# First attention: the scores of two heads in one step, with two half-height matmuls

## The chip, the cores and the metric

The kernel runs on one core of a Trainium2 chip. The time is the device time of one execution in microseconds, and lower is better. The core has a matrix engine (PE, TensorE), with its weight loads shown apart as PEld, two engines for elementwise work (DVE, ACT), a third, slower one (POOL), and queues that start DMA transfers (SP's and ACT's here). Each engine works through its own list of instructions in order and waits for the others through semaphores. Matmuls write to PSUM banks of 128 partitions by 512 floats; DVE and ACT read them from there.

## What is computed

One encoder layer for 1024 tokens of width 1024. A normed input goes through one projection whose columns feed two attentions, their outputs go through one output projection, and a gated MLP with a convolution of width 3 follows. The change touches only the scores of the first attention: windows of 128 tokens to either side, eight query heads of 64 dimensions, two key heads, and a learned sink per head:

```python
qa = partial_rope(qa.reshape(B, S, A_HEADS, HEAD_DIM), cos, sin)
ka = partial_rope(ka.reshape(B, S, A_KV_HEADS, HEAD_DIM), cos, sin)
...
s = jnp.einsum('bqgrd,bkgd->bgrqk', q_i, k_i).astype(jnp.float32) * scale
s = jnp.where(valid[None, None, None], s, -1e30)
m = jnp.maximum(jnp.max(s, axis=-1), sink_gr)
p = jnp.exp(s - m[..., None])
denom = jnp.sum(p, axis=-1) + jnp.exp(sink_gr - m)
o = jnp.einsum('bgrqk,bkgd->bgrqd', p.astype(v_i.dtype), v_i)
o = o / denom[..., None].astype(o.dtype)
```

## The kernel before

**Numbers in two parts.** Each operand of a matmul is split into a high part (a copy rounded to the matmul's type) and a low part (what the copy lost). A projection step is three matmuls, high weights by high input, high weights by low input, low weights by high input (`block`, L189 to L192).

**Scores.** A head has 64 dimensions, half of the array's 128 rows, so the high and the low part of a query are stacked in one tile of 128 partitions. A key is kept as two such tiles, one with high above low and one with low above high (`split_first_k` and `split_k`). `scores` (L398) multiplies the query's tile by both: the first matmul gives high by high plus low by low, the second the two mixed products, both into one bank `s`. Two heads come out of one projection tile; `split_first` (group 0) and `split_pair` (group 1) make their query tiles. In group 0 the second head has low above high already; in group 1 both have high above low, the halves being put in place by three copies on SP's queue.

**Tiling.** A unit is one key head (group `g` of four query heads) and one block `b` of 128 queries; there are 16 (`unit_window`, L461). Its scores are 128 by 384 for each head, or 128 by 256 in the first and last block of a group. A unit has four `q_step`s, one for a head, and two or three `t_step`s, one for a block of keys.

- A `q_step` takes a bank `s` (there are two), issues the two matmuls and calls `softmax`: DVE adds the mask and takes the minimum of the negated scores (L435), and the exponential on ACT (L443) is put off until the next call of `exponentials`, that is until the next `softmax` or the next `t_step`. After the second head of a pair, DVE inverts both sums (L445) and POOL scales both tiles (L447).
- A `t_step` transposes the four heads' blocks on TensorE (L483), splits the result into a high part on ACT (L457) and a low part on DVE (L458), and leaves a `v_step` of two matmuls (L489, L490), which is run one `t_step` later.

**Order.** TensorE's list is written out by hand: its instructions run in the order of the program. The loop over units takes the steps of the unit's transposes and, between them, the `q_step`s of the unit two further on (positions `EVA`). After each step it adds a share of other work (`fill`): projection products for later stages, in the number given by `RATES`. The order on DVE and ACT is left to a scheduler, with the softmax and the split of the transposes at raised priority.

Of the kernel before, what the change touches and what calls it, by code (L numbers as in the profile page):

```python
# [58 lines left out]
def hybrid_layer(tc, xT, w_first, w_in, w_out, w_gate, w_up, w_down, small, sink, rpb, consts, rope, out):  # L59
    nc = tc.nc  # L60
    with ExitStack() as ctx:
# [23 lines left out]
        def big(name, tag, dt=F32):  # L85
            return lpool.tile([128, S], dt, name=name, tag=tag, bufs=slots[tag])
# [4 lines left out]
        def bank(name, tag):  # L91
            return psum.tile([128, HALF], F32, name=name, tag=tag)

        f32 = lambda ap: ap.bitcast(F32)
# [21 lines left out]
        for name, dst, n in (("h", his, 2), ("h", his, 2), ("l", los, 2), ("l", los, 2), ("w", None, 2)):  # L116
            t = flat(big(name, "mix", F32R)[:, :], n)
# [47 lines left out]
        def behind(*names):  # L165

            stack = ExitStack()
            for n in names:
                stack.enter_context(tc.issue_after(mark[n].ins))
            return stack  # L170
# [108 lines left out]
        def split_pair(t):  # L279

            a, b = big("q", "op", F32R), big("q", "op", F32R)
            lo = t[:, :].bitcast(F32R)
            for h in range(2):
                nc.scalar.activation(a[:, tsl(h)], t[:, tsl(h)], AF.Copy, scale=-HD ** -0.5)
                nc.vector.scalar_tensor_tensor(lo[:, tsl(h)], t[:, tsl(h)], -HD ** -0.5, f32(a[:, tsl(h)]), op0=ALU.mult, op1=ALU.subtract)
            nc.sync.dma_start(f32(b[0:64, :]), f32(a[64:128, :]))
            nc.sync.dma_start(f32(b[64:128, :]), t[64:128])
            nc.sync.dma_start(f32(a[64:128, :]), t[0:64])
            return [a, b]

# [31 lines left out]
        def split_k(t, e):  # L322

            a, b = big("ka", "op", F32R), big("kb", "op", F32R)
            o = 64 - e
            nc.scalar.activation(a[e:e + 64], t[e:e + 64], AF.Copy)
            nc.sync.dma_start(f32(b[o:o + 64, :]), f32(a[e:e + 64, :]))
            nc.vector.tensor_tensor(b[e:e + 64], t[e:e + 64], f32(a[e:e + 64, :]), op=ALU.subtract)
            nc.sync.dma_start(f32(a[o:o + 64, :]), f32(b[e:e + 64, :]))
            return a, b  # L330

        later = []

# [28 lines left out]
        qa, ka, va, qb, kb, vb = {}, {}, {}, {}, {}, {}  # L362
# [32 lines left out]
        def near(b):  # L395
            return [c for c in (b - 1, b, b + 1) if 0 <= c < NB]

        def scores(q, k, b):  # L398
            cs = near(b)
            n = 128 * len(cs)  # L400
            ps = bank("s", "s")
            qs = q[:, b * 128:(b + 1) * 128]
            for i in range(2):
                nc.tensor.matmul(ps[:, 0:n], qs, k[i][:, cs[0] * 128:cs[0] * 128 + n].rearrange("p (s w) -> p w s", s=2), start=i == 0, stop=i == 1)  # L404
            return ps, n
# [4 lines left out]
        def pair_tile(spare=False):  # L410
            pairs[0] += 1
            if spare and pairs[0] % 7 in SPARE:
                return lpool.tile([128, 2, 386], F32, name="p", tag="mix", bufs=slots["mix"], padded_shape=[128, 2, 512])
            return apool.tile([128, 2, 386], F32, name="p", tag="p", bufs=5, padded_shape=[128, 2, 392])
# [3 lines left out]
        def exponentials(*order):  # L418
            while deferred:
                with tc.high_priority(offset=50):  # L420
                    deferred.pop(0)(*order)

        def softmax(st, j, ps, n, bias, nsink=None):

            exponentials()
            w = lambda ap: ap.rearrange("p (s w) -> p s w", s=2)
            p = st["p"]
            with tc.high_priority(offset=50):
                nm = spool.tile([128, 1], F32, name="nm")
                if j == 0:  # L430
                    st["sm"], st["n"] = spool.tile([128, 2], F32, name="sm"), [n, n]
                sm, st["n"][j] = st["sm"], n
                if nsink is not None and j == 0:
                    nc.gpsimd.tensor_copy(p[:, 0:2, n:n + 1], nsink.rearrange("p (j o) -> p j o", o=1))
                nc.vector.tensor_tensor_reduce(  # L435
                    out=w(p[:, j, 0:n]), in0=ps[:, 0:n].rearrange("p (w s) -> p s w", s=2), in1=bias, scale=1.0, scalar=3e38 if nsink is None else nsink[:, j:j + 1],
                    op0=ALU.add, op1=ALU.min, accum_out=nm)
                e = n if nsink is None else n + 1
                widths = list(st["n"])

                def finish(*order):
                    with behind(*order):
                        nc.scalar.activation(p[:, j, 0:e], p[:, j, 0:e], AF.Exp, bias=nm, scale=-1.0, accum_out=sm[:, j:j + 1])  # L443
                    if j == 1:
                        nc.vector.reciprocal(sm, sm)  # L445
                        for i, m in enumerate(widths):
                            mark["scaled"] = nc.gpsimd.tensor_scalar(p[:, i, 0:m], p[:, i, 0:m], sm[:, i:i + 1], 1.0, op0=ALU.mult, op1=ALU.mult)  # L447

                deferred.append(finish)
                if nsink is None:  # L450
                    exponentials()
# [9 lines left out]
        def unit_window(g, b):  # L461

            cs, n = near(b), 128 * len(near(b))
            ps4 = [None] * 4
            mask = w2(cst[:, K_MA + 128 * (cs[0] - b + 1):K_MA + 128 * (cs[-1] - b + 2)])
            st = {}

            def q_step(j):
                def go():
                    if j % 2 == 0:  # L470
                        st["p"] = pair_tile(True)
                    ps, _ = scores(qa[g, j // 2][j % 2], ka[g], b)
                    softmax(st, j % 2, ps, n, mask, nsink[:, 4 * g + j - j % 2:4 * g + j - j % 2 + 2])
                    ps4[j] = st["p"][:, j % 2, :]
                return go

            def t_step(i):
                def go():
                    if i == 0:
                        st["o"] = bank("o", "o")  # L480
                    pt = bank("pt", "pt")
                    for j in range(4):
                        nc.tensor.transpose(pt[:, j * 128:(j + 1) * 128], ps4[j][:, i * 128:(i + 1) * 128], ident)  # L483
                    ph, pl = split_pt(pt, HALF)
                    exponentials("high")

                    def v_step():
                        o, v = st["o"], va[g]
                        nc.tensor.matmul(o, v[:, cs[i], :], mv(ph[:, :]), start=i == 0, stop=False)  # L489
                        nc.tensor.matmul(o, v[:, cs[i], :], mv(pl[:, :]), start=False, stop=i == len(cs) - 1)  # L490
                        if i == len(cs) - 1:
                            leave()
                    return v_step
                return go

            def leave():
                ot = apool.tile([128, 2, 128], F32, name="ot", tag="ot", bufs=1, padded_shape=[128, 4, 128])
                o4 = pv(st["o"][:, :])
                halved = lambda ap: ap.rearrange("p (s w) -> p s w", s=2)
                for e in range(2):  # L500
                    me, other = slice(64 * e, 64 * e + 64), slice(64 - 64 * e, 128 - 64 * e)
                    nc.scalar.activation(ot[me].rearrange("p j (s w) -> p j s w", s=2), o4[other, e::2], AF.Copy)
                    for i in range(2):
                        if mix[2 * g + i] is None:
                            mix[2 * g + i] = big("mixa", "mix")
                        nc.vector.tensor_tensor(halved(mix[2 * g + i][me, b * 128:(b + 1) * 128]), o4[me, e + 2 * i], halved(ot[me, i, :]), op=ALU.add)

            return [q_step(j) for j in range(4)], [t_step(i) for i in range(len(cs))]
# [220 lines left out]
        nsink = cpool.tile([128, 8], F32, name="nsink")  # L729
# [5 lines left out]
        t = quarters(big("f", "mix"))  # L735
# [15 lines left out]
        for part in range(3):  # L751
            for p, ps in zip(first, banks):
                w, x = p.w[0], xg[0]
# [55 lines left out]
        def second_k():  # L809
            ka[1] = split_k(first[0].t, 64)  # L810
# [74 lines left out]
        for g in range(2):  # L885
            for b in range(NB):
                q, t = unit_window(g, b)
# [59 lines left out]
        for u in range(len(flat)):  # L947
            q, t, need, kind = flat[u]
# [123 lines left out]
        at = lambda k, h: h1[k][:, tsl(h)]  # L1072
# [48 lines left out]
        for h in range(2):  # L1121
            for d in range(KT):
                if h == 0 and d + 2 < KT:
                    wo.append(load_wo(d + 2, False))
                ps = bank("pj", ("o", "s", "pj")[(h * KT + d) % 3])
# [438 lines left out]
        for i, (p, j, c) in enumerate(order):  # L1564
# [4 lines left out]
            f, n = PARTS[c]  # L1569
# [5 lines left out]
            ps = banks[p, j]  # L1575
# [8 lines left out]
            q = i % 12  # L1584
# [18 lines left out]
        for k, cols in enumerate(quarters):  # L1603
            for j in (2, 3):
                ps = banks[6, j]
# [116 lines left out]
```

## Time and profile before

| | before |
|---|---|
| median of 3 runs | 1014.34 us (1014.22 to 1014.41) |
| span of the profiled execution | 1012.1 us |
| matmuls, weight loads | 5080, 5080 |
| HBM read, written | 104.11 MB, 28.58 MB |
| score matmuls of both attentions (L404) | 128 with each key tile |

The profiled execution's own time is not shown apart; its span, from the first to the last instruction, is 2.24 us under the median of the runs.

How to read a row: a group's row has line, engine, operation, output and inputs, shapes and count, then busy time in us, the mean of one in ns, and the idle time ahead with what ended it. A row of the timeline has start, duration, engine, line, operation and count. Matmuls are pipelined: a row's duration overlaps with the next one's, so the distance between two starts tells what a matmul takes of the stream.

### The profile page before, as it was taken

The numbers are of one execution on the slowest core, as the hardware profiler recorded it, in microseconds if no ns is written. First come the engines' busy times: TensorE is split into PE (matmuls) and PEld (weight loads), VectorE is DVE, ScalarE is ACT, GpSimd is POOL, SyncE is SP. The second block draws the span as 40 slices with busy tenths as digits, with TensorE's granted clock in tenths as the row PEclk, the third lists the DMA queues.
The fourth block names the chain that finished last, engine by engine and source line by source line (L and its number), as shares of the span: only waits on it lengthen the run. The fifth ranks groups of instructions, "written<-read, shape, count | busy, mean of one in ns | idle before, by whom it ended". The sixth has DMA issues, their size and how long they took to land.

```text
span 1012.1 us, 14835 instructions
## 1 busy us (share of the span) xinstructions
PE 1004.5 (99%) x5080; PEld 888.4 (88%) x5080; DVE 834.7 (82%) x1570; ACT 561.0 (55%) x1080; POOL 101.6 (10%) x186
## 2 busy tenths in 40 slices
PE   9999999999999999999999999999999999999997
PEld 8899898899899888888888888888888888888887
DVE  7899887768888799999987786786777678996675
ACT  8567776658687554565544443443444645554451
POOL 0233342222322100000000000000000000000001
PEclk9999999999999999999999999999999999999999
DMA  7223022333334366232552333323332799976654
GB/s 296 83 79 90 32 73 63 84 84 83 95 94 136 126 205 220 74 103 64 195 187 90 112 115 115 105 94 115 104 119 90 239 315 329 306 241 231 214 174 177
DMA packets 68524, 145.46 MB, mean 144 GB/s; under 512 B 8280, under 2 KB 18784, under 8 KB 68448
## 3 DMA queue, kind: packets, MB, share of 16 engines
q1 hardware_dynamic: 58360, 119.27, 36.9%
q10 hardware_dynamic: 10088, 25.24, 6.4%
q8 instruction: 40, 0.66, 0.3%
q14 instruction: 36, 0.29, 0.1%
HBM read 104.11 MB, written 28.58 MB: 131 GB/s over the span
## 4 chain that ended last, share of the span: by engine, by line
PE 93%; DVE 3%; ACT 2%; DMA 1%; issue 1%; SPq 0%; DVEq 0%; ACTq 0%
PE x L1059 8%; PE x L1057 8%; PE x L1058 8%; PE pj L190 7%; PE pj L192 7%; PE pj L191 7%; PE dn L1059 7%; PE dn L1058 7%; PE dn L1057 7%; PE y L1059 4%; PE y L1057 4%; PE y L1058 4%; PE s L404 3%; PE pt L483 2%; PE z L1057 2%; PE z L1059 2%
## 5 line engine op out<-in xcount | busy, mean ns | idle before, releaser
L1057 PE MATMUL x<-hg,whi 128*128 128x512 f32 x352 | 133.5, 379 | 0.0
L1058 PE MATMUL x<-hg,whi 128*128 128x512 f32 x352 | 133.4, 379 | 0.0
L1059 PE MATMUL x<-hg,wlo 128*128 128x512 f32 x352 | 133.4, 379 | 0.0
L1057 PE MATMUL dn<-xd,whi 128*128 128x512 f32 (+1 forms) x330 | 120.8, 366 | 0.0
L1058 PE MATMUL dn<-xd,whi 128*128 128x512 f32 (+1 forms) x330 | 120.5, 365 | 0.0
L1059 PE MATMUL dn<-xd,wlo 128*128 128x512 f32 (+1 forms) x330 | 120.5, 365 | 0.0
L1031 ACT ACTIVATE whi<-ws 128x512 fp32r<-128x512 f32 (+1 forms) x100 | 60.9, 623 | 76.0 <-DVE ws L1171 14.5
L443 ACT ACTIVATE p<-p,nm 128x385 f32<-128x385 f32 (+3 forms) x128 | 75.2, 588 | 45.8 <-DVE nm L435 43.1
L190 PE MATMUL pj<-xgh,whi 128*128 128x512 f32 x245 | 99.7, 407 | 0.2 <-DVE v L346 0.2
L447 POOL TENSOR_SCALAR p<-p,sm 128x384 f32<-128x384 f32 (+1 forms) x128 | 76.4, 610 | 195.9 <-DVE sm L445 161.7
L191 PE MATMUL pj<-xgl,whi 128*128 128x512 f32 x245 | 92.9, 379 | 0.0
L192 PE MATMUL pj<-xgh,wlo 128*128 128x512 f32 x245 | 92.9, 379 | 0.0
L1031 ACT ACTIVATE whi<-raw 128x512 fp32r<-128x512 f32 (+1 forms) x102 | 61.2, 612 | 49.9 <-PE x L1058 14.9
L1032 DVE TENSOR_TENSOR wlo<-ws,whi 128x512 fp32r<-128x512 f32 (+1 forms) x100 | 66.8, 683 | 20.0 <-ACT whi L1031 19.6
L458 DVE TENSOR_TENSOR pl<-pt,ph 128x384 fp32r<-128x384 f32 (+2 forms) x108 | 63.4, 587 | 17.5 <-ACT ph L457 16.5
L1057 PEld LDWEIGHTS x<-hg,whi 128*128 128x128 f32 x352 | 66.5, 189 | 9.4
L1058 PEld LDWEIGHTS x<-hg,whi 128*128 128x128 f32 x352 | 66.5, 189 | 9.4
L1059 PEld LDWEIGHTS x<-hg,wlo 128*128 128x128 f32 x352 | 66.5, 189 | 9.4
L1032 DVE TENSOR_TENSOR wlo<-raw,whi 128x512 fp32r<-128x512 f32 (+1 forms) x102 | 66.8, 672 | 6.2 <-ACT whi L1031 6.1
L1532 POOL TENSOR_TENSOR h<-h,wide 128x256 f32<-128x256 f32 x4 | 2.8, 731 | 671.2 <-ACT wide L1528 671.2
L457 ACT ACTIVATE ph<-pt 128x384 fp32r<-128x384 f32 (+2 forms) x108 | 55.4, 513 | 26.3 <-PE pt L483 14.2
L1057 PEld LDWEIGHTS dn<-xd,whi 128*128 128x128 f32 x330 | 62.5, 189 | 7.8
(276 smaller groups left out, 2504.2 us busy)
## 6 DMA issues: line engine op xcount, KB each, us to landing
xd<-x SPq DMA_DIRECT2D x77, 256.0 KB, 4.9
raw<-in_w_down_dram SPq DMA_DIRECT2D x72, 256.0 KB, 4.6
raw<-in_w_gate_dram SPq DMA_DIRECT2D x22, 512.0 KB, 3.5
raw<-in_w_up_dram SPq DMA_DIRECT2D x22, 512.0 KB, 3.8
x<-c ACTq DMA_DIRECT2D x22, 512.0 KB, 2.8
raw<-in_w_in_dram SPq DMA_DIRECT2D x30, 256.0 KB, 2.8
raw<-in_w_down_dram SPq DMA_DIRECT2D x36, 192.0 KB, 4.2
x<-t ACTq DMA_DIRECT2D x11, 512.0 KB, 2.6
```

Of the source, the lines that this page charges most:

```text
L190: nc.tensor.matmul(ps, w[0], mv(x[0][:, tsl(h)]), start=first, stop=False)
L191: nc.tensor.matmul(ps, w[0], mv(x[1][:, tsl(h)]), start=False, stop=False)
L192: nc.tensor.matmul(ps, w[1], mv(x[0][:, tsl(h)]), start=False, stop=last)
L443: nc.scalar.activation(p[:, j, 0:e], p[:, j, 0:e], AF.Exp, bias=nm, scale=-1.0, accum_out=sm[:, j:j + 1])
L447: mark["scaled"] = nc.gpsimd.tensor_scalar(p[:, i, 0:m], p[:, i, 0:m], sm[:, i:i + 1], 1.0, op0=ALU.mult, op1=ALU.mult)
L457: mark["high"] = nc.scalar.activation(ph[:, 0:n], ps[:, 0:n], AF.Copy)
L458: mark["rest"] = nc.vector.tensor_tensor(pl[:, 0:n], ps[:, 0:n], f32(ph[:, 0:n]), op=ALU.subtract)
L1031: nc.scalar.activation(hi, src, AF.Copy)
L1032: nc.vector.tensor_tensor(lo, src, f32(hi[:, :, :]), op=ALU.subtract)
L1057: nc.tensor.matmul(ps, w[0], x[0], start=first and i == 0, stop=False, skip_group_check=True)
L1058: nc.tensor.matmul(ps, w[0], x[1], start=False, stop=False, skip_group_check=True)
L1059: nc.tensor.matmul(ps, w[1], x[0], start=False, stop=last and i == len(ws) - 1, skip_group_check=True)
```

## The change

The four heads of a unit are now scored in two steps of two heads, and the odd `q_step`s return at once. `scores_of_two` takes both banks `s`. It first issues high by high for both heads: for the even head with rows 0 to 63 of its query tile and of the first key tile, for the odd head with rows 64 to 127 of its query tile and of the second. Then each head gets its two mixed products with one matmul of full height. The product of both low parts, which was in the first matmul, is left out. The query tiles of odd heads in group 1 are now low above high, and `split_k` returns its two tiles in the other order. `softmax` runs for both heads in the same step and flushes the put-off exponentials only ahead of the first.

```diff
-            nc.sync.dma_start(f32(b[0:64, :]), f32(a[64:128, :]))
-            nc.sync.dma_start(f32(b[64:128, :]), t[64:128])
+            nc.sync.dma_start(f32(b[64:128, :]), f32(a[64:128, :]))
+            nc.sync.dma_start(f32(b[0:64, :]), t[64:128])
             nc.sync.dma_start(f32(a[64:128, :]), t[0:64])
...
-            return a, b
+            return b, a
...
-        def softmax(st, j, ps, n, bias, nsink=None):
-
-            exponentials()
+        def scores_of_two(q, k, b):
+
+            cs = near(b)
+            at, n = cs[0] * 128, 128 * len(cs)
+            qs = [t[:, b * 128:(b + 1) * 128] for t in q]
+            ks = [t[:, at:at + n].rearrange("p (s w) -> p w s", s=2) for t in k]
+            both = [bank("s", "s") for _ in range(2)]
+            for e, r in enumerate((slice(0, 64), slice(64, 128))):
+                nc.tensor.matmul(both[e][:, 0:n], qs[e][r], ks[e][r], start=True, stop=False)
+            for e in range(2):
+                nc.tensor.matmul(both[e][:, 0:n], qs[e], ks[1 - e], start=False, stop=True)
+            return both, n
+
+        def softmax(st, j, ps, n, bias, nsink=None, flush=True):
+
+            if flush:
+                exponentials()
...
             def q_step(j):
                 def go():
-                    if j % 2 == 0:
-                        st["p"] = pair_tile(True)
-                    ps, _ = scores(qa[g, j // 2][j % 2], ka[g], b)
-                    softmax(st, j % 2, ps, n, mask, nsink[:, 4 * g + j - j % 2:4 * g + j - j % 2 + 2])
-                    ps4[j] = st["p"][:, j % 2, :]
+                    if j % 2:
+                        return
+                    st["p"] = pair_tile(True)
+                    both, _ = scores_of_two(qa[g, j // 2], ka[g], b)
+                    for e in range(2):
+                        softmax(st, e, both[e], n, mask, nsink[:, 4 * g + j:4 * g + j + 2], e == 0)
+                        ps4[j + e] = st["p"][:, e, :]
                 return go
```

The second attention keeps `scores` with one head and two matmuls of full height.

## Prediction

> **What bounds the kernel now.** I read the page first (busy shares, chain), then the stage in which the changed lines run, then its waits, and last the instructions one by one.
>
> ```profile
> span 1012.1 us, 14835 instructions
> ...
> PE 1004.5 (99%) x5080; PEld 888.4 (88%) x5080; DVE 834.7 (82%) x1570; ACT 561.0 (55%) x1080; POOL 101.6 (10%) x186
> ...
> PE 93%; DVE 3%; ACT 2%; DMA 1%; issue 1%; SPq 0%; DVEq 0%; ACTq 0%
> ```
>
> TensorE is never short of work: 99% busy, and 93% of the chain that ended last. The timeline places the first attention's scores from 52.3 us to the end of their minima at 167.6 us. There the busy times (PE, PEld, DVE, ACT, POOL) and all that TensorE's weight loads waited for, for another engine, are:
>
> ```profile
> 52.30:167.60 115.30, 115.30 (x659) 103.52 (x659) 102.97 (x301) 86.14 (x221) 41.56 (x87) 1.00 0.27 71
> PEld s L404 <- DVE nm L435: 0.4, 1, 0.4
> PEld o L490 <- DVE pl L458: 0.3, 1, 0.3
> ```
>
> PE is busy in all 115.30 us, at full clock, and its loads waited 0.7 us in all. So a microsecond of matmul stream taken out of this stage comes out of the span, as long as the other engines keep up. DVE is the one to watch: 102.97 of 115.30 us, 89%.
>
> **What a score matmul costs.** The groups of the stage with their shapes (busy us, mean ns) give the counts; the instructions by time (start, duration) give the price.
>
> ```profile
> L404 PE MATMUL s<-ka,q 128*128 128x384 f32 x48 | 16.7, 348 | 0.0
> L404 PE MATMUL s<-ka,q 128*128 128x256 f32 x16 | 4.7, 294 | 0.0
> ```
>
> ```profile
> 52.34 0.27 PE L404 MATMUL s<-ka,q 128*128 128x256 f32 x1
> 52.45 0.28 PE L404 MATMUL s<-kb,q 128*128 128x256 f32 x1
> ...
> 57.78 0.38 PE L192 MATMUL pj<-xgh,wlo 128*128 128x512 f32 x1
> 57.99 0.33 PE L404 MATMUL s<-ka,q 128*128 128x384 f32 x1
> 58.16 0.33 PE L404 MATMUL s<-kb,q 128*128 128x384 f32 x1
> 58.32 0.38 PE L190 MATMUL pj<-xgh,whi 128*128 128x512 f32 x1
> ```
>
> Durations overlap, so the price is the distance between starts: two 384-column matmuls take 58.32 - 57.99 = 0.33 us, 0.165 each; two of 256 start 0.11 apart (52.34, 52.45). A 512-column matmul lasts 0.38 but gives way after 0.21 to 0.22; the other 0.165 is a tail that the next matmul covers.
>
> The weight loads have a price of their own:
>
> ```profile
> 58.00 0.19 PEld L404 LDWEIGHTS s<-kb,q 128*128 128x128 f32 x1
> ...
> 64.81 0.19 PEld L404 LDWEIGHTS s<-ka,q 128*128 128x128 f32 x1
> 64.92 0.19 PEld L404 LDWEIGHTS s<-kb,q 128*128 128x128 f32 x1
> ```
>
> ```profile
> 64.47 0.60 PE L483 MATMUL pt<-cst,p 128*128 128x128 f32 x4
> 64.83 0.41 PE L404 MATMUL s<-ka,q 128*128 128x384 f32 x1
> 65.08 0.33 PE L404 MATMUL s<-kb,q 128*128 128x384 f32 x1
> ...
> 159.42 0.60 PE L483 MATMUL pt<-cst,p 128*128 128x128 f32 x4
> ```
>
> Each load starts as the matmul before its own starts (58.00 beside 57.99): one load ahead, no more. Behind the four transposes the loads come 0.11 us apart (64.81, 64.92), and the first score matmul begins in truth only when the second load does. So 0.11 is the smallest distance of two loads seen here.
>
> **The change, part by part.** 48 and 16 head blocks make 24 wide pairs and 8 narrow ones. A pair has four matmuls and four weight loads before and after. Two of the matmuls now use rows 0 to 63 and rows 64 to 127 of the array, with different banks as outputs. If they stream at the same time, a pair takes three slots instead of four.
>
> No row of this trace has a matmul of half height, so its price is bounded. At one end the second half is hidden entirely: 24 x 0.165 + 8 x 0.11 = 4.84 us saved. At the other it streams after the first: nothing saved. In between stands its weight load. Of the even heads, 21 stand behind a 512-column matmul (14 wide, 7 narrow), whose 0.21 us hold two loads of 0.11 if the second half's load may also start early, its rows being free; 11 stand right behind transposes (10 wide, 1 narrow, the first at 64.47, the last at 159.42), where loads already queue and the second half starts 0.11 late. That gives 14 x 0.165 + 7 x 0.11 + 10 x (0.165 - 0.11) = 2.31 + 0.77 + 0.55 = 3.63 us. If the second load never starts before the first half does, only 24 x 0.055 = 1.32 us are left. I take 3.63: loads are the one resource that the rows show to be serial, and I assume that streams on separate rows are not.
>
> By the Trainium skill, TensorE: Matmul & The Clock Gate, section Part 3: Packing small matmuls, matmuls on separate row groups run at the same time, about 4 ns apart; by it alone the sum is close to the upper end, 4.84 - 32 x 0.004 = 4.71 us (an estimate from that page). No run here shows it yet.
>
> The steps move as well. The odd head's scores are issued with the even head's, and its own step does nothing; fill work between steps is handed out per event as before, so PE's list keeps its length. What is new is a wait: a pair asks for both score banks at once, so the minimum of the odd head before must be read too.
>
> ```profile
> L435 DVE CUSTOM_DVE_ANT_0 p<-s,cst,nsink 128x384 f32<-128x384 f32 x48 | 28.9, 608 | 0.5
> L435 DVE DVE_READ_ACCUMULATOR2_ANT nm<- 128x1 f32 x64 | 5.3, 82 | 0.0
> L443 ACT ACTIVATE p<-p,nm 128x385 f32<-128x385 f32 x48 | 29.5, 614 | 6.3 <-DVE nm L435 5.5 <-DVE sm L445 0.3 <-POOL p L447 0.2
> ```
>
> ```profile
> 53.42 0.48 DVE L435 CUSTOM_DVE_ANT_0 p<-s,cst,nsink 128x256 f32<-128x256 f32 x1
> 54.29 0.69 DVE L253 TENSOR_TENSOR t<-pj,rstd 128x512 f32<-128x512 f32 x1
> 54.73 0.27 PE L404 MATMUL s<-ka,q 128*128 128x256 f32 x1
> ...
> 102.80 0.19 PEld L404 LDWEIGHTS s<-ka,q 128*128 128x128 f32 x1 [0.40 <-DVE nm L435]
> ...
> 160.28 0.48 DVE L435 CUSTOM_DVE_ANT_0 p<-s,cst,nsink 128x256 f32<-128x256 f32 x1 [0.84 <-PE s L404]
> 163.12 0.27 PE L404 MATMUL s<-ka,q 128*128 128x256 f32 x1
> ```
>
> For the 31 pair starts after the first (first 54.73, last 163.12) I took the time from the end of the minimum two heads back to the start of the scores, in the order of before, and took off one more minimum, 0.61 + 0.08 = 0.69 us. Four come out negative, by 0.94 us together; the worst is 102.80, where PE waits already. If one more DVE step of 0.69 us lies between the two minima, the sum is 6.32 us. And below nothing: the present wait of 0.4 us could go. I take 0.94, the row order being the nearest evidence. Behind the waiting score load stand the projection products and the o matmuls, the whole PE list; nothing else is late first.
>
> At nothing I cost the rest. The two exponentials of a pair come one behind the other on ACT, which is 86.14 of 115.30 us busy, and their scaled result is transposed two units later (a unit is 115.30 / 16 = 7.2 us); that cover gone, each would delay a transpose by its own 0.61 us. The three copies that build the second group's queries go to other halves with the same sizes, on SP's queue in the same order, 8 us ahead of their first reader:
>
> ```profile
> 98.77 0.46 SPq L288 DMA_DIRECT2D q<-t  x1
> 107.16 0.27 PE L404 MATMUL s<-ka,q 128*128 128x256 f32 x1
> ```
>
> The first pair needs both query tiles at once. Their low halves are made by 49.57, before 52.34:
>
> ```profile
> 47.10 2.47 DVE L296 SCALAR_TENSOR_TENSOR q<-t,q 64x1024 fp32r<-64x1024 f32 x2 [0.45 <-ACT q L295]
> ```
>
> **Sum.** -3.63 + 0.94 = -2.69 us: a span of 1009.4. The median of the runs shown, 1014.34, is 2.24 us above the profiled span; with the same 2.24 around it the time is 1011.6 us, 0.27% less. A measurement of this kernel tells about 0.2% (2.0 us) from no change, so this is only just outside.
>
> **Rivals.** *The halves do not run side by side.* The second streams behind the first, or its load starts with it: savings of 0 or 1.32 us against waits of 0 to 0.94, so 1013.0 to 1015.3 us, and 1014.3 as its middle. For it speaks the one load ahead in all rows; against it that the two halves share no rows and no bank.
>
> *The array empties when the height changes.* Place: TensorE, at the step from full to half height and back, 2 x 32 = 64 times. Price: if the tail must run out, the uncovered 0.165 us from the 512-column row, 64 x 0.165 = 10.6 us; less 3.63 that is +6.9, so 1021.3 us. It decides from 3.63 / 64 = 0.057 us a switch; with an uncovered weight load of 0.11 at each as well it is 64 x 0.275 - 3.63 = +14.0, 1028.3. Against it stands the one change of kind in the trace, transposes to matmuls at 64.47 to 65.08: the distances there are explained by loads of 0.11 alone, with no tail of 0.165. But both have full height. The Trainium skill, TensorEngine Tiling (Array Packing), Key Properties under Tiling Modes, says that changing the tiling mode, not just the tile, drains TensorE; it gives no price, and no run here shows it yet. By that rule this rival is the result.
>
> *DVE becomes the bound through the banks.* Each pair meets one more DVE step of 0.69 between its minima: 6.32 us of waits less 3.63, +2.7, 1017.0 us. For it speaks 89% of DVE, and more if the stage shrinks; against it that the two minima become ready together and have the same priority.
>
> **How the numbers follow.** Forecast 0.47, with its own range from 1009.5 (4.84 saved, no new wait) to 1012.3; no overlap 0.23; emptying array 0.22; banks 0.08. Faster is the forecast, 0.47; within 0.2% is the first rival, 0.23; slower are the other two, 0.30. The range reaches from 1009.3 to 1021.5 and leaves out the costlier half of the emptying array and a little below.
>
> **What will show it.** Right: the starts of the two half-height matmuls lie at most 0.11 us apart, the pair's first matmul to the next instruction is about 0.50 us for a wide pair (now 0.66), and PE's waits for the minimum stay near 1 us. First rival: the halves 0.165 apart, 0.66 for the pair. Emptying array: gaps ahead of the first half and ahead of the first full matmul behind it, without a releaser. Banks: PE or its loads wait on L435's successor for several us. Wrong in another way would be waits of o matmuls for the split of the transposes, which would mean that the new order on ACT and DVE costs more than I gave it.

## The result, and the profile after

The changed kernel takes 1021.97 us (median of 4 runs, 1021.12 to 1022.48) against 1014.28 (4 runs, 1013.78 to 1014.41): 7.7 us more, a ratio of 1.0078 with a 95% interval of 1.0064 to 1.0093. The prediction was 1011.6 us, 2.7 us less. The measured time lies just above its range, at the place of the second rival (1021.3 us).

The page of the changed kernel, the lines that answer to those shown first:

```profile
span 1020.4 us, 14838 instructions
...
PE 1013.0 (99%) x5080; PEld 884.3 (87%) x5080; DVE 835.4 (82%) x1570; ACT 558.0 (55%) x1080; POOL 100.7 (10%) x186
...
PE 96%; DVE 2%; DMA 1%; issue 0%; ACT 0%; DVEq 0%
```

The number of matmuls and loads is the same, PE is still at 99%, and it is busy 8.5 us longer (1013.0 after 1004.5). TensorE does not wait longer for others; it takes longer itself. Where, the busy times in two stretches show, up to 175.0 us, where the first attention's scores and minima are done, and behind it:

```profile
52.30:175.00 122.70, 122.70 (x657) 98.36 (x656) 103.71 (x300) 83.41 (x222) 40.63 (x87) 1.00 0.26 67
175.00:1020.00 845.00, 839.04 (x4187) 740.76 (x4185) 689.01 (x1210) 439.72 (x815) 52.29 (x82) 1.00 0.45 151
```

The weight loads' waits in the first stretch (us in total, times, the longest):

```profile
PEld s L431 <- issue: 4.8, 17, 0.3
PEld s L433 <- issue: 4.2, 24, 0.2
PEld s L431 <- DVE v L346: 1.0, 3, 0.3
PEld s L431 <- DVE sm L459: 1.0, 3, 0.3
PEld s L431 <- DVE mixa L522: 0.7, 3, 0.3
...
PEld s L431 <- DVE nm L449: 0.2, 1, 0.2
```

Before, 659 matmuls took 115.30 us here; now 657 take 122.70. The clock is still 1.00. The first score of the second attention, which the change does not touch, dates the loss: 167.90 us before, 176.06 after, 8.2 us later. Not all of that arose in the stage: the projection matmul ahead of the first scores starts at 52.13 us before and at 52.74 after, 0.61 us later already. It ran late from the start, where in this execution some of the first matmuls start 0.43 us apart in place of 0.22: the first matmul of L190 starts at 7.82 us, before at 6.87. That is not the change's doing, for in run 6 below, with the same instructions there, it starts at 6.86. The stage itself grew by 7.55 us (176.06 - 52.74 against 167.90 - 52.13), and behind it nothing changed (from that score to the end of the span it is 844.3 us, 844.2 before).

```profile
167.90 0.27 PE L404 MATMUL s<-ka,q 128*128 128x256 f32 x1
```

```profile
176.06 0.27 PE L404 MATMUL s<-ka,q 128*128 128x256 f32 x1
```

New are idle stretches ahead of the weight loads of the two score lines (L431 the halves, L433 the full ones), the sign that the prediction named for the emptying array. The releasers named there, if any, change from case to case while the length stays 0.2 or 0.3 us. A constant gap with a changing name belongs to the waiting engine; the name is only the last thing that happened before. So the one gap that bears the name of the minimum (nm), 0.17 us at 83.61, is no wait for it: a pair of loads behind transposes idles as long at 66.65 under another name. Of the waits that the prediction priced at 0.94 us, the only one that could be left is a second half that starts 0.19 us behind the first, at 91.42.

One wide pair of the changed kernel behind a projection matmul, first TensorE, then its weight loads:

```profile
58.96 0.38 PE L192 MATMUL pj<-xgh,wlo 128*128 128x512 f32 x1
59.27 0.43 PE L431 MATMUL s<-ka,q 64*128 64x384 f32 x1
59.27 0.43 PE L431 MATMUL s<-kb,q 64*128 64x384 f32 x1
59.63 0.43 PE L433 MATMUL s<-kb,q 128*128 128x384 f32 x1
59.89 0.33 PE L433 MATMUL s<-ka,q 128*128 128x384 f32 x1
60.06 0.38 PE L190 MATMUL pj<-xgh,whi 128*128 128x512 f32 x1
```

```profile
59.27 0.18 PEld L431 LDWEIGHTS s<-ka,q 64*128 64x128 f32 x1 [0.33 <-DVE v L346]
59.27 0.18 PEld L431 LDWEIGHTS s<-kb,q 64*128 64x128 f32 x1
59.63 0.19 PEld L433 LDWEIGHTS s<-kb,q 128*128 128x128 f32 x1 [0.17 <-issue]
59.73 0.19 PEld L433 LDWEIGHTS s<-ka,q 128*128 128x128 f32 x1
```

Both halves start at 59.27, and so do their loads: they do run side by side. But the projection matmul gives way after 0.215 us, at 59.175, and the loads begin only at 59.27, about 0.09 later; none began under the matmul, as each did before. The halves can stream only when their loads are in, about 0.11 us on (in run 2 below, two half-height loads on the same rows start 0.11 apart). They stream about 0.163 us (in run 1 below, four matmuls of 384 columns take 0.65, 61.02 to 61.67) and end at 59.54; then again 0.09 of nothing, a load from 59.63, and the next full matmul streams from 59.73. So **a border between full and half height costs about 0.09 us of nothing and 0.11 us of uncovered load**. Together they are 0.198 us, half of what the pair takes beyond the projection matmul and three streams (1.10 - 0.215 - 3 x 0.163 = 0.396). That the array empties in the 0.09 us is our reading: the trace shows only that no load starts then, and the ends of matmuls in it are modelled.

From the projection matmul to the instruction behind the pair it is 60.06 - 58.96 = 1.10 us; before, 0.21 + 4 x 0.165 = 0.87. Behind transposes the loss is the same: from the transposes to the instruction behind a wide pair it is 67.44 - 66.12 = 1.32 us, and in run 1 below, at full height, 71.84 - 70.75 = 1.09. A narrow pair:

```profile
52.74 0.38 PE L192 MATMUL pj<-xgh,wlo 128*128 128x512 f32 x1
53.05 0.37 PE L431 MATMUL s<-ka,q 64*128 64x256 f32 x1
53.05 0.37 PE L431 MATMUL s<-kb,q 64*128 64x256 f32 x1
53.36 0.38 PE L433 MATMUL s<-kb,q 128*128 128x256 f32 x1
...
53.68 0.38 PE L190 MATMUL pj<-xgh,whi 128*128 128x512 f32 x1
```

It takes 0.94 us, where 0.21 + 4 x 0.11 = 0.65 stood. For all pairs that is 24 x 0.23 + 8 x 0.29 = 7.8 us, which is the result (7.7 by the medians, 7.55 in the stage).

### The profile page after: what moved, and what is told of

The parts are those of the page before. It is cut to its first block, busy times and chain, and to the rows that moved or that the text cites. A ratio compares the mean times of both kernels' runs of the same rounds, so it can differ in the third digit from the quotient of the medians.

```text
span 1020.4 us, 14838 instructions
## 1 busy us (share of the span) xinstructions
PE 1013.0 (99%) x5080; PEld 884.3 (87%) x5080; DVE 835.4 (82%) x1570; ACT 558.0 (55%) x1080; POOL 100.7 (10%) x186
## 4 chain that ended last, share of the span: by engine, by line
PE 96%; DVE 2%; DMA 1%; issue 0%; ACT 0%; DVEq 0%
PE pj L190 8%; PE pj L191 8%; PE pj L192 8%; PE x L1075 7%; PE x L1073 7%; PE x L1074 7%; PE dn L1075 6%; PE dn L1073 6%; PE dn L1074 6%; PE y L1073 4%; PE y L1075 4%; PE y L1074 4%; PE pt L499 2%; PE z L1075 2%; PE z L1073 2%; PE z L1074 2%
## 5 line engine op out<-in xcount | busy, mean ns | idle before, releaser
L190 PE MATMUL pj<-xgh,whi 128*128 128x512 f32 x245 | 100.1, 408 | 0.2 <-DVE v L346 0.2
L1075 PEld LDWEIGHTS dn<-xd,wlo 128*128 128x128 f32 x330 | 62.5, 189 | 8.1 <-DVE wlo L1048 0.5
```

Of the source, the lines that this page charges most:

```text
L190: nc.tensor.matmul(ps, w[0], mv(x[0][:, tsl(h)]), start=first, stop=False)
L1075: nc.tensor.matmul(ps, w[1], x[0], start=False, stop=last and i == len(ws) - 1, skip_group_check=True)
```

## The experiments

The theory, "border": the time went into the 64 borders. Its rivals: "order", that it went into the new order and the two banks at once; and "half height is slow", that a half-height matmul is dear in itself, wherever it stands. Each run has runs of the kernel before beside it on the same chip; the difference is that of the medians, in us. The column "stage" leaves out what differs elsewhere: it is what the trace of one execution gained, against 115.8 us before, from the projection matmul ahead of the first scores to the first score of the second attention.

| run | median, us | before beside it | difference | stage | ratio, 95% interval |
|---|---|---|---|---|---|
| changed kernel | 1021.97 | 1014.28 | +7.7 | +7.6 | 1.0078 (1.0064 to 1.0093) |
| 1 full height, two heads in a step | 1014.76 | 1013.80 | +1.0 | +0.4 | 1.0010 (1.0000 to 1.0019) |
| 2 both halves on the same rows | 1026.35 | 1013.80 | +12.6 | +12.0 | 1.0122 (1.0105 to 1.0139) |
| 3 the halves issued twice | 1027.99 | 1013.80 | +14.2 | +13.2 | 1.0141 (1.0126 to 1.0156) |
| 4 the halves apart | 1038.62 | 1013.80 | +24.8 | +24.5 | 1.0244 (1.0229 to 1.0260) |
| 5 all half | 1017.00 | 1013.78 | +3.2 | +2.9 | 1.0033 (1.0021 to 1.0044) |
| 6 halves last | 1021.94 | 1013.78 | +8.2 | +7.6 | 1.0081 (1.0065 to 1.0098) |
| 7 high keys, full height | 1007.28 | 1013.96 | -6.7 | -8.0 | 0.9932 (0.9918 to 0.9945) |

**1. Full height, everything else of the change.**

```diff
-            for e, r in enumerate((slice(0, 64), slice(64, 128))):
+            for e, r in enumerate((slice(0, 128), slice(0, 128))):
                 nc.tensor.matmul(both[e][:, 0:n], qs[e][r], ks[e][r], start=True, stop=False)
```

> The step of two heads stays, with both banks taken at once, but all four matmuls have full height (the product of both low parts is back). Theory 'border': what costs is the change between full and half height on TensorE; per border about 0.09 us of emptying and 0.107 us of weight load that nothing covers, 64 borders, less 4.8 us of stream saved. None of it is left here: 1014.3 us, up to 1015.3 with the 0.94 us of bank waits of the prediction. Rival 'order': the cost is that of the new order and of two banks at once: about 1022 us, as in the changed kernel.

+1.0 us against +7.7. "Order" falls as the main cause: with the same steps and banks and no half-height matmul nearly all of the loss is gone. The 1.0 us left is near the 0.94 that the prediction had for the bank waits, but the trace shows only a part of it under that name. The weight loads' waits for DVE in the stage:

```profile
PEld s L431 <- DVE nm L449: 0.8, 3, 0.4
```

Before, they were 0.4 us, so 0.4 us are new, and the stage grew by the same 0.4. Where the rest of the 1.0 us lies is not shown, and by the interval the 1.0 itself could be anything from 0.0 to 1.9. A slower TensorE meets fewer of these waits (0.19 us at most in the changed kernel), so they hardly add to the borders.

**2. Both halves on rows 0 to 63.**

```diff
-            for e, r in enumerate((slice(0, 64), slice(64, 128))):
+            for e, r in enumerate((slice(0, 64), slice(0, 64))):
```

> As the changed kernel, but both half-height matmuls use rows 0 to 63, so the odd head's first product is taken from its low part and the key's low part (another product than the reference's). Theory 'border' with halves that run side by side on separate rows: here they cannot, the second streams behind the first: 24 x 0.163 + 8 x 0.11 = 4.8 us more than the changed kernel, 1026.8 us. Rival 'no overlap': the halves of the changed kernel gained nothing from separate rows: 1022 us, no change.

+12.6, 4.9 us more than the changed kernel's +7.7; 4.8 was expected of halves that overlap only on separate rows. By the stage alone it is 4.5 us. So the change did what it says: one slot of stream per pair was saved. In the timeline of this run the second half comes 0.26 us behind the first:

```profile
59.62 0.43 PE L431 MATMUL s<-ka,q 64*128 64x384 f32 x1
59.88 0.32 PE L431 MATMUL s<-kb,q 64*128 64x384 f32 x1
60.14 0.43 PE L433 MATMUL s<-kb,q 128*128 128x384 f32 x1
```

Those 0.26 are the first half's own load, 0.1, and its 0.16 of stream. The loads show the first of the two:

```profile
59.62 0.18 PEld L431 LDWEIGHTS s<-ka,q 64*128 64x128 f32 x1 [0.33 <-DVE v L346]
59.73 0.19 PEld L431 LDWEIGHTS s<-kb,q 64*128 64x128 f32 x1
```

**3. The halves issued twice.**

```diff
-            for e, r in enumerate((slice(0, 64), slice(64, 128))):
-                nc.tensor.matmul(both[e][:, 0:n], qs[e][r], ks[e][r], start=True, stop=False)
+            for i, e, r in ((i, e, slice(64 * e, 64 * e + 64)) for i in range(2) for e in range(2)):
+                nc.tensor.matmul(both[e][:, 0:n], qs[e][r], ks[e][r], start=i == 0, stop=False)
```

> As the changed kernel, but each pair of half-height matmuls is issued twice in a row, so that high by high counts twice in the scores. Theory 'border': no further border, one slot more, the loads of the second pair covered by the stream of the first: 24 x 0.163 + 8 x 0.11 = 4.8 us more, 1026.8 us. Rival 'half height is slow': every half-height pair pays its uncovered load and its emptying, 0.36 us wide and 0.31 us narrow as between the first half and the next full matmul now: 24 x 0.36 + 8 x 0.31 = 11.1 us more, 1033.1 us.

+14.2, 6.5 more than the changed kernel, between the two expectations (4.8 and 11.1) and nearer to the theory. The instructions of a wide pair decide: the second pair of loads starts under the stream of the first halves, and from the first halves to the full matmul it is 60.16 - 59.64 = 0.52 us in place of 0.36. One slot, no further border.

```profile
59.64 0.43 PE L431 MATMUL s<-ka,q 64*128 64x384 f32 x1
...
59.90 0.32 PE L431 MATMUL s<-ka,q 64*128 64x384 f32 x1
59.91 0.32 PE L431 MATMUL s<-kb,q 64*128 64x384 f32 x1
60.16 0.43 PE L433 MATMUL s<-kb,q 128*128 128x384 f32 x1
```

```profile
59.64 0.18 PEld L431 LDWEIGHTS s<-kb,q 64*128 64x128 f32 x1
59.74 0.19 PEld L431 LDWEIGHTS s<-ka,q 64*128 64x128 f32 x1
```

Of the 1.7 us left over, waits of the halves explain about 0.9. Two wide pairs take longer than their like (1.86 us where the others take 1.26, and 1.96 where they take 1.48), 1.08 us together, against 0.19 in the changed kernel; in both, the second half's load waits for the minimum:

```profile
PEld s L431 <- DVE nm L449: 1.4, 5, 0.4
```

The whole 1.4 us can't be put down to it, since a load at a border idles 0.17 or 0.33 us under any name. By the stage alone the run is 5.7 us above the changed kernel, and those 0.9 are about all that is left over.

**4. The halves apart: half, full, half, full.**

```diff
             for e, r in enumerate((slice(0, 64), slice(64, 128))):
                 nc.tensor.matmul(both[e][:, 0:n], qs[e][r], ks[e][r], start=True, stop=False)
-            for e in range(2):
                 nc.tensor.matmul(both[e][:, 0:n], qs[e], ks[1 - e], start=False, stop=True)
```

> As the changed kernel with the same four matmuls per pair, but in the order half, full, half, full: each half-height matmul stands alone between full ones. Theory 'border': four borders a pair in place of two, 64 more at 0.195 us = 12.5 us, and the halves no longer side by side, 4.8 us: 17.3 us more than the changed kernel, 1039.3 us. Rivals 'order' or 'half height is slow' without a price for borders: 4.8 us more at most, 1026.8 us.

+24.8, 17.1 more than the changed kernel, where the theory gave 17.3 and its rivals 4.8 at most. The same four matmuls, only in another order: 4.8 us for the lost overlap, the other 12.3 for 64 more borders, 0.19 us each. The steps are 0.36 us apart throughout:

```profile
60.13 0.43 PE L431 MATMUL s<-ka,q 64*128 64x384 f32 x1
60.49 0.43 PE L432 MATMUL s<-kb,q 128*128 128x384 f32 x1
60.85 0.43 PE L431 MATMUL s<-kb,q 64*128 64x384 f32 x1
61.21 0.43 PE L432 MATMUL s<-ka,q 128*128 128x384 f32 x1
```

**5. All four at half height, two slots.**

```diff
-            for e in range(2):
-                nc.tensor.matmul(both[e][:, 0:n], qs[e], ks[1 - e], start=False, stop=True)
+            for e, r in enumerate((slice(0, 64), slice(64, 128))):
+                nc.tensor.matmul(both[e][:, 0:n], qs[e][r], ks[1 - e][r], start=False, stop=True)
```

> As the changed kernel, but the two mixed matmuls are half-height too, on the rows of their head, so that both heads' second products also run side by side; the product of low queries with high keys is left out. Theory 'border': still two borders a pair, but two slots in place of three: 4.8 us less than the changed kernel, 1017.2 us, and still 2.9 us above the kernel before, although it streams half of the score columns that the kernel before does: the two borders, 32 x 0.39 = 12.5 us, are more than the two slots, 9.6 us. Rival 'half height is slow' (each half-height pair pays 0.36 us wide, 0.31 narrow): a pair then takes 0.72 and 0.62 us in place of the changed kernel's 0.79 and 0.63 from the first half on, so 1020 us.

+3.2; 2.9 was expected of the theory, some 6 of "half height is slow". Two slots in place of four, and it is still slower than the kernel before: two borders a pair are more than two slots.

**6. The full-height matmuls first, the halves last.** The two loops of `scores_of_two` change places, with start and stop.

> As the changed kernel, but the two full-height matmuls come first and the two half-height ones last, so that the borders lie between the step's own full matmuls and the halves, and between the halves and whatever follows. Theory 'border': the price goes with the number of borders, not with what stands on their sides: 1022 us, within 1 us. Rival 'entry wait': part of the cost is the first half's wait for the two score banks at the start of the step, where no load can run ahead; with a full-height matmul first that wait is as small as before, and 2 us or more come back: 1020 us or less.

+8.2 against +7.7, no difference that the intervals allow to be told. In the stage both grew by 7.6 us. What stands on the sides of the border does not matter here, and the first half's wait for the banks is no part of the cost that can be seen.

**7. A slot saved without a border.** The kernel before, with one full-height score matmul for each head of the first attention.

```diff
-            a, b = big("ka", "op", F32R), big("kb", "op", F32R)
-            up, down = slice(0, 64), slice(64, 128)
...
+            a = big("ka", "op", F32R)
+            for part in (slice(0, 64), slice(64, 128)):
+                nc.scalar.activation(a[part], t[0:64], AF.Copy)
+            return [a]
...
-            for i in range(2):
+            for i in range(len(k)):
```

> The kernel before, at full height throughout, with one score matmul per head in place of two: the key tile holds the high part in both halves, so the stacked query gives high by high plus low query by high key; the products with the low part of the keys are left out (the kernel with all halves left out those with the low part of the queries). Theory: the stage is paid by TensorE slots, and a slot saved without a border is saved in full: 48 x 0.163 + 16 x 0.11 = 9.6 us less than before, 1004.2 us against 1013.8. Rival: DVE, busy for 103 of the stage's 115.3 us before, becomes the bound in a stage of 105.7 us and gives back 3 us or more in waits of TensorE for the minimum or the split of the transposes: 1007 us or more.

-6.7 us, faster than both kernels (ratio to the kernel before 0.9932, 0.9918 to 0.9945), but it computes less than either: with the products it also leaves out the making of the keys' low parts, three subtractions on DVE and one copy by DMA. It streams as many slots as run 5 and is 9.9 us below it by the differences (3.2 + 6.7), 12.5 being the price of run 5's borders. Of the 9.6 us, 2.9 did not arrive, 1.6 of them in the stage, which lost 8.0. There the waits of TensorE's loads for score minima and for the split of the transposes grew; these rows of run 7 stood at 0.4, 0.3 and nothing before:

```profile
PEld s L399 <- DVE nm L430: 1.1, 3, 0.5
...
PEld o L485 <- DVE pl L453: 0.7, 3, 0.3
...
PEld o L484 <- ACT ph L452: 0.4, 1, 0.4
```

They make 1.5 us of the 1.6. Another wait that grew, from 0.2 us, lies at 266.99, over 100 us behind the stage, and nothing shows that the shorter stage causes it:

```profile
PE pj L190 <- DVE v L341: 0.8, 1, 0.8
```

So the run's rival holds in part: with a shorter stage the other engines begin to be late. This is read from the trace and wasn't tested, and the rest of the 2.9 us is not placed.

## Why the prediction was wrong

- **What bounds the kernel**: right. TensorE's own stream sets the time, and every result here is the sum of its slots and gaps, within 3 us.
- **One slot of four saved**: right, and too small in the sum. The prediction took 3.63 us, since it let the second half's load queue behind the first. The loads of separate rows start together (59.27 and 59.27), also behind transposes (66.65 and 66.65), so the upper end, 4.84 us, holds; run 2 gives 4.9.
- **The step that failed** is the height change costed at nothing: "Against it stands the one change of kind in the trace, transposes to matmuls at 64.47 to 65.08". That row shows that full-height instructions of different kinds follow each other without a gap. It says nothing about a change of height, which no row of the kernel before has. A price stood in the text (0.165 us a border, 0.275 with a load), and I took nothing, by an analogy. The runs showed about 0.198 us at each of the 64 borders: run 1, without borders, loses 1.0 us in place of 7.7, and run 4, with 64 more and the overlap gone, loses another 17.1, of which 12.3 are the borders' by the theory.
- **The rival that came true** was priced at 64 x 0.165 - 3.63 = +6.9 us. That this comes so near is partly luck, for both terms were off and the errors cancel in part: the border costs about 0.198, not as one tail of 0.165 but as 0.09 of nothing and 0.11 of load; the saving is 4.84. 64 x 0.198 - 4.84 = +7.8, measured +7.7. The dearer form of the rival (+14.0) had both parts, a tail and a load, and mis-sized the tail, 0.165 against 0.09. The break-even of the prediction, 0.057 us a border, becomes 4.84 / 64 = 0.076, and the border is 2.6 times that.
- The Trainium skill, TensorEngine Tiling (Array Packing), Key Properties, has it that changing the tiling mode drains TensorE. This trace agrees, with about 0.09 us at each change in which nothing is loaded, and adds a load of 0.11 us that isn't hidden.
- The Trainium skill, TensorE: Matmul & The Clock Gate, Part 3, has matmuls on separate row groups start some 4 ns apart. The trace agrees as far as its two digits go: the halves start within 0.01 us.
- **Bank waits**: 0.94 us was too much. For the order alone run 1 lost 1.0 us, but in its stage the waits for the minimum grew by 0.4 only; in the changed kernel at most 0.19 is left, and a later TensorE that finds its banks free would explain that. The other edits at nothing held: nothing moved behind the stage.
- **The chances**: the rival had 0.22 and the range ended at 1021.5, below the 1021.97 measured. An unknown cost with 64 places and a rule that speaks for it deserved more than an analogy with one row.

## What to carry to other kernels

Count the borders, not the matmuls: a change between full and half height costs about 0.2 us here each way, so a visit to half height pays only if it saves more than 0.4 us, which is 2.4 slots of 384 columns; this change saved one. Two half-height matmuls on separate rows, with outputs in separate banks, do run in the time of one, loads included. So longer stretches at half height should pay, but no run here has one that does: run 5, with two slots saved for each visit, is still 3.2 us slower than the kernel before. Sharing a visit among three wide pairs would need six score banks at once in the way this kernel is built, and wasn't tried.

## What the runs showed of the hardware

Under a full-height matmul the next load starts with the matmul (58.00 beside 57.99 before) and is hidden. Across a change of height no load starts until about 0.09 us behind the end of the stream, so the hidden load becomes visible, and this is the larger part of the price (0.11 of 0.198). Within half height the hiding works again (59.74 in run 3). Half-height loads on separate rows start at the same time (59.27 and 59.27), on the same rows 0.11 us apart (59.62 and 59.73 in run 2).
